# Low parts of the recurrent layer's weights made in the two feed-forward stages and kept in DRAM, that layer's elementwise products on VectorE alone

## The chip, the core and the metric

The kernel runs on one core of one Trainium2 chip. The metric is the device time of one execution in microseconds (us), the median of three runs. TensorE is called PE, VectorE DVE, ScalarE ACT, GpSimd POOL and SyncE SP in the profile's rows; PEld is PE's loading of weights.

## The reference

A chain of four layers on one sequence of 512 tokens with 1024 features, all in float32:

```
x = x + 0.5 * swiglu(rms_norm(x), gate, up, down)       # first feed-forward, 2816 wide
x = x + token_mixer(rms_norm(x))                        # short convolution beside a WKV-7 scan
x = x + 0.5 * swiglu(rms_norm(x), gate, up, down)       # second feed-forward
x = rms_norm(x)
x = x + fourier_attention(rms_norm(x)) @ w_out          # FFT mixing beside grouped attention
h = rms_norm(x)                                         # the recurrent layer (RG-LRU)
xr, gate = split(h @ w_in, 2)                           # 2048 each
xc = conv_b + sum_j shift(xr, j) * conv_w[j]            # 4 taps
for each direction:                                     # forward and reverse
    r = sigmoid(xc_block @ w_a + b_a);  i = sigmoid(xc_block @ w_x + b_x)    # 16 blocks of 128
    a = exp(-8 * r * softplus(-lam));   u = sqrt(1 - a*a) * i * xc
    hseq = scan(a, u)                                   # h[t] = a[t] * h[t-1] + u[t]
x = x + ((forward + reverse) * silu(gate)) @ w_out
y = rms_norm(x)
```

## The kernel before

Features lie on the 128 partitions, the 512 tokens along the free axis; a tile is 128x512 (256 KB). A weight group is 128x1024 (512 KB) and makes one 128x512 result out of eight tiles of input. Every product is made of three matmuls, to hold float32's precision on operands of a shorter type: `mm3` multiplies the high part of the weights with the high and the low part of the data, and the low part of the weights with the high part of the data. So `wload` does for each group: a DMA of the group into a tile `raw` (3 buffers), a cast into `wh` (4 buffers; on ACT or DVE, as the planner finds), and on DVE the difference `raw - wh` into `wl` (4 buffers). A group feeds 24 matmuls of 512 columns. `split` does the same to data (`h`, `l`).

The order of the instructions is made by a planner in the program (`Rec.schedule`): every operation is recorded with a cost, and a list scheduler plays the engines forward and takes, on each, the ready operation with the lowest priority number (its place in the program plus a bias). It holds back what lies more than 800 operations ahead of the oldest one not yet issued (`room`) and what finds no buffer free. An operation recorded by `nc.tt` may go to DVE or POOL, one by `nc.copy` to ACT or DVE, wherever it would end sooner by the planner's costs. To an operation of DVE or POOL that begins while the other is on SBUF, the planner adds 0.65 of the overlap. Each engine then runs its instructions strictly in that order, and all DMAs are issued by SP in one queue.

The four layers stand one after another in `Net.all`: `ffn`, `mixer`, `ffn`, `even` (Fourier and attention), `odd` (recurrent). In `ffn`, 22 pairs of groups (`_g`, `_u`) and 24 groups (`_d`) follow each other, in chunks of 8, 8 and 6 pairs with 8 groups behind each.

In `odd` a loop goes over eight blocks of 256 recurrent features. For a block, `conv` multiplies two groups of `o_in` and applies the taps (tiles `xc`), `gates` multiplies one group of `gw`, and makes, for two halves and two directions, the gates (Sigmoid, Tanh, Exp and Sqrt on ACT), products on the tiles `t` and the scan, and adds the directions; `silu` multiplies two more groups of `o_in` (tiles `z`), and `gated` multiplies and splits the result. `gates` of a block runs beside `conv` of the next. From the fifth block on, two groups of `o_out0` (`part`) stand in every turn; `out` uses the eight groups of `o_out1` at the end. That is 32 + 8 + 16 = 56 weight groups.

Of the kernel before, what the change touches and what calls it, by code (L numbers as in the profile page):

```python
# [8 lines left out]
F32 = mybir.dt.float32  # L9
F32R = mybir.dt.float32r  # L10
AF = mybir.ActivationFunctionType
ALU = mybir.AluOpType
# [221 lines left out]
class Rec:  # L234
# [22 lines left out]
    def add(self, eng, fn, args, kw, alts=()):  # L257
        o = Op()
# [35 lines left out]
        o.table = f if fn == "activation" and f in _FUNCS else None  # L294
        o.prio = o.seq + self.bias
        o.succ = []
        self.ops.append(o)
# [14 lines left out]
    def schedule(self, hold=2000.0):  # L312
# [30 lines left out]
        front = 0  # L343
# [18 lines left out]
        def room(o):  # L362
            if o.seq > front + self.ahead.get(o.fn, self.ahead[None]):
                return False
            for nm in o.touch:
                if nm in first and nm not in held:
                    t = self.tag[nm][0]
                    if free[t] <= 0:
                        return False
                    f = first[nm]  # L370
                    if f > front and use[t][front:f].max() >= self.size[t]:
                        return False
            return True
# [16 lines left out]
        while len(order) < n or ends:  # L390
# [14 lines left out]
            for e in engs:  # L405
# [85 lines left out]
                elif e in ports and o.port:  # L491
                    f = "gpsimd" if e == "vector" else "vector"
                    c += 0.65 * max(0.0, min(ports[f] - now, c))
                    ports[e] = now + c
# [146 lines left out]
class Net:  # L641
    def __init__(self, tc, a, ctx, wbufs=(3, 4, 4), slots=76):
# [10 lines left out]
        self.slots = slots  # L653
        self.late = 60
        nc = self.nc
        self.cst = self.cp.tile([128, _NC], F32, name="cst")
# [79 lines left out]
    def group(self, name, g):  # L736
        ap = self.a[name]
        return self.wload(ap[g], ap.shape[1:])

    def group_tm(self, g):  # L740
# [82 lines left out]
    def ffn(self, n):  # L823
# [3 lines left out]
        for ch, nk in enumerate((8, 8, 6)):  # L827
            hs = []
            for gi in range(g0, g0 + nk):
# [11 lines left out]
                nc.gpsimd.tensor_tensor(u, u, t, ALU.mult)  # L841
                hs.append(self.split(u))
            g0 += nk
            for m in range(8):
                wd = self.group(f"{n}_d{ch}", m)
                ps = self.P()
                self.gemm(ps, wd, hs)
                xm = self.x[m]
                nc.vector.scalar_tensor_tensor(xm, ps, 0.5, xm, op0=ALU.mult, op1=ALU.add)


# [683 lines left out]
    def odd(self):  # L1535
# [41 lines left out]
        def gates(g, xcs):  # L1577

            gw = self.wload(self.a["gw"][g], (128, 2, 4, 128))
            us = [(m, d, d * 16 + 2 * g + m) for m in range(2) for d in range(2)]  # L1580
# [13 lines left out]
            for (m, d, i), r, ig in zip(us, rs, igs):  # L1594
                th = self.T()
                A.activation(th, r, AF.Tanh, scale=c8[:, i:i + 1])
                nc.tt(ig, ig, xcs[m][0], ALU.mult)
                ths.append(th)
# [6 lines left out]
            for (m, d, i), r, ig, th in zip(us, rs, igs, ths):  # L1605
                A.activation(th, th, AF.Sqrt)
                nc.tt(ig, ig, th, ALU.mult)
                h = th
# [4 lines left out]
            for m in range(2):  # L1613
                nc.tt(ths[2 * m], ths[2 * m], ths[2 * m + 1], ALU.add)
            return ths[0], ths[2]

        def silu(b):
# [6 lines left out]
            A.activation(s, z, AF.Sigmoid)  # L1624
            nc.tt(s, s, z, ALU.mult)
            return s

        def gated(zs, hsum):
            out = []
            for s, h in zip(zs, hsum):  # L1630
                nc.tt(s, s, h, ALU.mult)
                out.append(self.split(s))
            return out
# [83 lines left out]

    def all(self):
        n = len(self.rec.ops)
        self.ffn("ffn1")  # L1720

        w = [o for o in self.rec.ops[n:] if o.fn == "dma_start"][:2]
        l = [o for o in self.rec.ops[:n] if o.fn == "dma_start"]
        for i, o in enumerate([l[0], w[0]] + l[1:3] + [w[1]] + l[3:]):
            o.prio = i - 100.0
        self.mixer()
        self.ffn("ffn2")
        self.even()
        self.odd()
# [21 lines left out]
```

## Time and profile before

| | before |
|---|---|
| median of three runs | 2006.84 us (2006.65 to 2007.8) |
| profiled execution | 2006.84 us |
| its span, first to last instruction | 2005.1 us |
| time outside the span | 1.74 us |
| mean granted TensorE clock | 0.979 of 2.4 GHz |
| PE busy in the span | 95% |
| first feed-forward, mixer, second feed-forward, Fourier and attention, recurrent layer | about 0 to 390, 390 to 830, 830 to 1195, 1195 to 1600, 1600 to 2005 us |

The profile shows one execution, instruction by instruction. An engine's row by stretch says how long it was busy, and how many instructions it began; a PE that is never idle at the full clock begins 443 matmuls of 512 columns in 100 us. All operations carry the line of one helper (L550, in the kernel after the change L551), so groups are told apart by the names of their tiles.

### The profile page before, as it was taken

To read this page: it belongs to the slowest core of one execution; us is meant where nothing else is said; L and a number is where in the kernel's file an instruction comes from. 1 tells how busy PE (TensorE), PEld (TensorE's weight loads), DVE (VectorE), ACT (ScalarE), POOL (GpSimd) and SP (SyncE) were. 2 spreads that over 40 slices of the span, in tenths; PEclk is the share of its full clock that TensorE was granted. 3 is DMA by queue.
4 is the path that set the end of the run, shared out by engine and by line. 5 is a ranking of instruction groups with operands and counts; after the bars stand their busy time and mean duration, and the time that the engine had idled before them with its cause. 6 is when DMAs were issued, how large, how long until landed. Compare 5 with 4: busy or idle time off the path is not lost.

```text
span 2005.1 us, 24763 instructions
## 1 busy us (share of the span) xinstructions
PE 1904.9 (95%) x9756; PEld 1559.7 (78%) x9756; DVE 1345.2 (67%) x2041; ACT 789.3 (39%) x1118; POOL 488.2 (24%) x307
## 2 busy tenths in 40 slices
PE   7999999999999998999999998999999999788997
PEld 6888888877777776788888886888998887577777
DVE  7434434779898964754344357754678868999995
ACT  5222222543442422432222234332465546865661
POOL 2201101231101301412011025100101026566563
PEclk9999999999999989999999999999999999898999
DMA  5332332432322311423223223222211131222221
GB/s 179 102 99 90 112 103 87 150 97 83 97 79 64 95 56 32 142 90 105 95 94 108 89 92 117 76 64 93 86 53 43 64 95 63 74 85 84 85 74 64
DMA packets 83013, 178.57 MB, mean 89 GB/s; under 512 B 27216, under 2 KB 39760, under 8 KB 82896
## 3 DMA queue, kind: packets, MB, share of 16 engines
q1 hardware_dynamic: 82896, 176.99, 27.9%
q8 instruction: 76, 1.25, 0.3%
q14 instruction: 41, 0.34, 0.1%
HBM read 169.10 MB, written 7.86 MB: 88 GB/s over the span
## 4 chain that ended last, share of the span: by engine, by line
PE 68%; DVE 23%; issue 4%; ACT 2%; POOL 1%; DMA 1%; POOLq 0%; SPq 0%; DVEq 0%; ACTq 0%
PE pm L550 65%; DVE t L550 5%; DVE wl L550 5%; PE pw L550 4%; DVE q L550 2%; DVE xc L550 2%; DVE l L550 2%; DVE u L550 1%; DVE wh L550 1%; DVE s L550 1%; ACT t L550 1%; DVE z L550 1%; POOL t L550 1%; ACT L550 0%; DVE x L550 0%
## 5 line engine op out<-in xcount | busy, mean ns | idle before, releaser
L550 PE MATMUL pm<-xh,wl 128*128 128x512 f32 x1488 | 556.7, 396 | 30.9 <-DVE wl L550 30.8
L550 ACT CAST wh<-raw 128x1024 fp32r<-128x1024 f32 (+1 forms) x255 | 264.6, 1039 | 816.5 <-PE pm L550 743.8
L550 PE MATMUL pm<-xh,wh 128*128 128x512 f32 x1488 | 557.3, 397 | 12.2 <-ACT xh L550 8.2
L550 PE MATMUL pm<-xl,wh 128*128 128x512 f32 x1488 | 555.8, 396 | 0.0
L550 POOL TENSOR_TENSOR t<-t,t 128x512 f32<-128x512 f32 x110 | 216.4, 1978 | 947.7 <-DVE t L550 772.7
L550 DVE TENSOR_TENSOR wl<-raw,wh 128x1024 fp32r<-128x1024 f32 (+1 forms) x303 | 400.1, 1323 | 22.8 <-ACT wh L550 18.5
L550 PEld LDWEIGHTS pm<-xh,wl 128*128 128x128 f32 x1488 | 282.1, 190 | 96.5 <-DVE wl L550 37.8
L550 PEld LDWEIGHTS pm<-xh,wh 128*128 128x128 f32 x1488 | 283.2, 191 | 75.3 <-ACT xh L550 8.2
L550 PEld LDWEIGHTS pm<-xl,wh 128*128 128x128 f32 x1488 | 282.8, 190 | 61.3 <-issue 1.1
L550 PE MATMUL pm<-h,wh 128*128 128x512 f32 (+2 forms) x844 | 311.2, 388 | 13.9 <-DVE t L550 8.0
L550 PE MATMUL pm<-h,wl 128*128 128x512 f32 (+2 forms) x844 | 310.8, 387 | 6.2 <-DVE wl L550 6.2
L550 PE MATMUL pm<-l,wh 128*128 128x512 f32 (+2 forms) x844 | 310.1, 386 | 2.1 <-DVE l L550 2.1
L550 DVE TENSOR_TENSOR t<-pm,rstd 128x512 f32<-128x512 f32 x146 | 99.5, 687 | 218.5 <-PE pm L550 216.3
L550 PEld LDWEIGHTS pm<-h,wh 128*128 128x128 f32 (+1 forms) x844 | 158.7, 190 | 48.7 <-DVE t L550 8.9
L550 PEld LDWEIGHTS pm<-h,wl 128*128 128x128 f32 (+1 forms) x844 | 159.3, 190 | 39.5 <-DVE wl L550 8.1
L550 PEld LDWEIGHTS pm<-l,wh 128*128 128x128 f32 (+1 forms) x844 | 158.7, 190 | 35.6 <-DVE l L550 5.1
L550 ACT ACT_TABLE_LOAD x82 | 105.2, 1283 | 19.1 <-DMA x<-xT 6.1
L550 DVE SCALAR_TENSOR_TENSOR x<-pm,x 128x512 f32<-128x512 f32 x48 | 33.1, 689 | 118.6 <-PE pm L550 118.4
L550 POOL TENSOR_TENSOR acc<-acc,sq 128x512 f32<-128x512 f32 x42 | 68.3, 1635 | 136.2 <-ACT sq L550 135.9
L550 DVE TENSOR_TENSOR x<-x,pm 128x512 f32<-128x512 f32 (+1 forms) x44 | 27.5, 635 | 63.9 <-PE pm L550 63.8
L550 DVE TENSOR_TENSOR_SCAN t<-t,t 128x512 f32<-128x512 f32 x32 | 66.6, 2130 | 2.4 <-POOL t L550 2.4
L550 ACT ACTIVATE t<-t 128x512 f32<-128x512 f32 x100 | 60.4, 629 | 14.5 <-DVE t L550 9.0
(246 smaller groups left out, 2246.4 us busy)
## 6 DMA issues: line engine op xcount, KB each, us to landing
raw<-ffn_g SPq DMA_DIRECT2D x44, 512.0 KB, 3.7
raw<-ffn_u SPq DMA_DIRECT2D x44, 512.0 KB, 3.5
raw<-w_in SPq DMA_DIRECT2D x42, 512.0 KB, 3.7
raw<-ffn_d SPq DMA_DIRECT2D x32, 512.0 KB, 3.6
raw<-o_in SPq DMA_DIRECT2D x32, 512.0 KB, 3.5
raw<-e_f SPq DMA_DIRECT2D x16, 512.0 KB, 3.6
raw<-e_out SPq DMA_DIRECT2D x16, 512.0 KB, 3.5
raw<-o_out SPq DMA_DIRECT2D x16, 512.0 KB, 3.5
```

The source lines that it names most:

```text
L550: o.ins = getattr(getattr(self.nc, o.eng), o.fn)(*o.args, **o.kw)
```

## The change

Fifty-six low parts are made ahead. `put_low` takes a group of the recurrent layer, does the whole of `wload` on it (in the buffers of the running stage, its priority put back by 40 places) and stores the tile `wl` in a DRAM tile `low`. In the first feed-forward stage 28 groups are treated so (4 of `o_in`, the 8 of `gw`, the 16 of `o_out`), in the second the other 28 of `o_in`: one behind each of the first 20 pairs, and one behind every second `_d` group of the first two chunks. In `odd`, `group` then finds the low part in `self.low` and calls `wload_low`: two DMAs (`raw`, and `wl` from DRAM, the second held to 200 operations ahead), the cast into `wh`, and no difference on DVE. The high part is still cast there.

All products of `odd` that `nc.tt` recorded are recorded on DVE alone. POOL keeps the additions of squares in the two norms. And the planner adds 0.95 instead of 0.65 of an overlap of DVE and POOL, in all layers.

```diff
-            if o.seq > front + self.ahead.get(o.fn, self.ahead[None]):
+            if o.seq > front + (o.far or self.ahead.get(o.fn, self.ahead[None])):
...
-                    c += 0.65 * max(0.0, min(ports[f] - now, c))
+                    c += 0.95 * max(0.0, min(ports[f] - now, c))
...
+        if (name, g) in self.low:
+            return self.wload_low(ap[g], self.low.pop((name, g)), ap.shape[1:])
         return self.wload(ap[g], ap.shape[1:])
+
+    def wload_low(self, ap, low, shape):
+        nc = self.nc
+        raw = self.wt(shape, F32, "raw")
+        nc.sync.dma_start(out=raw, in_=ap)
+        l = self.wt(shape, F32R, "wl")
+        nc.sync.dma_start(out=l.bitcast(F32), in_=low).far = 200
+        h = self.wt(shape, F32R, "wh")
+        nc.copy(h, raw)
+        return h, l
+
+    def put_low(self, n):
+        for name, g in self.later[:n]:
+            ap = self.a[name]
+            self.rec.bias = self.behind
+            _, l = self.wload(ap[g], ap.shape[1:])
+            t = self.dp.tile(list(ap.shape[1:]), F32, name=self.nm("low"))
+            self.nc.sync.dma_start(out=t, in_=l.bitcast(F32))
+            self.rec.bias = 0
+            self.low[name, g] = t
+        self.later = self.later[n:]
...
                 hs.append(self.split(u))
+                if gi < 20:
+                    self.put_low(1)
...
                 nc.vector.scalar_tensor_tensor(xm, ps, 0.5, xm, op0=ALU.mult, op1=ALU.add)
+                if ch < 2 and m % 2 == 1:
+                    self.put_low(1)
...
-            gw = self.wload(self.a["gw"][g], (128, 2, 4, 128))
+            gw = self.group("gw", g)
...
-                nc.tt(ig, ig, xcs[m][0], ALU.mult)
+                V.tensor_tensor(ig, ig, xcs[m][0], ALU.mult)
...
-                nc.tt(ig, ig, th, ALU.mult)
+                V.tensor_tensor(ig, ig, th, ALU.mult)
...
-                nc.tt(ths[2 * m], ths[2 * m], ths[2 * m + 1], ALU.add)
+                V.tensor_tensor(ths[2 * m], ths[2 * m], ths[2 * m + 1], ALU.add)
...
-            nc.tt(s, s, z, ALU.mult)
+            V.tensor_tensor(s, s, z, ALU.mult)
...
-                nc.tt(s, s, h, ALU.mult)
+                V.tensor_tensor(s, s, h, ALU.mult)
...
+        odd = [("o_in", g) for g in range(32)] + [("gw", g) for g in range(8)]
+        odd += [(f"o_out{h}", g) for h in range(2) for g in range(8)]
         n = len(self.rec.ops)
+        self.later = odd[28:]
         self.ffn("ffn1")
...
         self.mixer()
+        self.later = odd[:28]
         self.ffn("ffn2")
```

What this does to the order of the instructions is seen at three places; a name like `wl2701` is one buffer's use, the number behind `_` is the program's.

SP's queue in the first feed-forward stage, before: the loads of two groups for each pair, and nothing between them.

```order
L550 DMA raw90_165<-ffn1_u 128x1024
L550 DMA raw98_173<-ffn1_g 128x1024
L550 DMA raw102_177<-ffn1_u 128x1024
L550 DMA raw110_185<-ffn1_g 128x1024
L550 DMA raw114_189<-ffn1_u 128x1024
L550 DMA raw122_197<-ffn1_g 128x1024
```

The same place in the changed kernel:

```order
L551 DMA low101_176<-wl100_175 128x1024
L551 DMA raw114_189<-gw 128x1024
L551 DMA raw134_209<-ffn1_g 128x1024
L551 DMA raw138_213<-ffn1_u 128x1024
L551 DMA low117_192<-wl116_191 128x1024
L551 DMA raw130_205<-gw 128x1024
L551 DMA raw150_225<-ffn1_g 128x1024
L551 DMA raw154_229<-ffn1_u 128x1024
L551 DMA low133_208<-wl132_207 128x1024
```

Between two pairs stand the store of a low part and the load of the next group to be treated: four DMAs where there were two.

DVE in the third turn of the recurrent layer's loop, before, around the scans (printed here as SCALAR_TENSOR_TENSOR of two tiles t):

```order
L550 CAST wh2477_2565<-raw2476_2564 128x1024
L550 SCALAR_TENSOR_TENSOR t2409_2497<-t2394_2482,t2396_2484 128x512
L550 TENSOR_TENSOR t2427_2515<-pm2426_2514,rstd2285_2365 128x512
L550 TENSOR_TENSOR wl2478_2566<-raw2476_2564,wh2477_2565 128x1024
L550 SCALAR_TENSOR_TENSOR t2410_2498<-t2398_2486,t2400_2488 128x512
L550 SCALAR_TENSOR_TENSOR t2411_2499<-t2402_2490,t2404_2492 128x512
L550 SCALAR_TENSOR_TENSOR t2412_2500<-t2406_2494,t2408_2496 128x512
L550 TENSOR_TENSOR z2363_2451<-z2363_2451,t2409_2497 128x512
```

And in the changed kernel:

```order
L551 TENSOR_TENSOR t2620_2708<-t2620_2708,t2633_2721 128x512
L551 SCALAR_TENSOR_TENSOR t2633_2721<-t2618_2706,t2620_2708 128x512
L551 TENSOR_TENSOR t2624_2712<-t2624_2712,t2634_2722 128x512
L551 TENSOR_TENSOR t2628_2716<-t2628_2716,t2635_2723 128x512
L551 SCALAR_TENSOR_TENSOR t2634_2722<-t2622_2710,t2624_2712 128x512
L551 SCALAR_TENSOR_TENSOR t2635_2723<-t2626_2714,t2628_2716 128x512
L551 TENSOR_TENSOR t2632_2720<-t2632_2720,t2636_2724 128x512
L551 TENSOR_TENSOR t2633_2721<-t2633_2721,t2634_2722 128x512
L551 SCALAR_TENSOR_TENSOR t2636_2724<-t2630_2718,t2632_2720 128x512
L551 TENSOR_TENSOR z2646_2734<-z2646_2734,t2645_2733 128x512
L551 TENSOR_TENSOR t2635_2723<-t2635_2723,t2636_2724 128x512
L551 TENSOR_TENSOR z2652_2740<-z2652_2740,t2651_2739 128x512
```

The difference `wl` is gone from between the scans, and the products `t<-t,t` and `z<-z,t`, which stood on POOL, stand among them. In the whole program DVE's row of instructions has 104 products more, and POOL's 104 fewer.

SP's queue in the recurrent layer before, where a group of `gw` stands behind four of `o_in`:

```order
L550 DMA raw2449_2537<-gw 128x1024
L550 DMA raw2476_2564<-o_in 128x1024
L550 DMA raw2482_2570<-o_in 128x1024
L550 DMA raw2492_2580<-o_in 128x1024
L550 DMA raw2500_2588<-o_in 128x1024
L550 DMA raw2508_2596<-gw 128x1024
```

And at that place in the changed kernel:

```order
L551 DMA raw2716_2804<-o_in 128x1024
L551 DMA raw2724_2812<-o_in 128x1024
L551 DMA raw2732_2820<-gw 128x1024
L551 DMA raw2759_2847<-o_in 128x1024
L551 DMA wl2701_2789<-low1641_1718 128x1024
L551 DMA wl2707_2795<-low1653_1730 128x1024
L551 DMA wl2717_2805<-low1441_1518 128x1024
L551 DMA wl2725_2813<-low1453_1530 128x1024
L551 DMA wl2733_2821<-low165_240 128x1024
L551 DMA raw2765_2853<-o_in 128x1024
```

Four loads of `raw` stand ahead of five loads of `wl`; the first of these, `wl2701`, belongs to the group whose `raw2700` was loaded before all rows shown. Such runs stand at four places in the loop's first five turns; later the two kinds alternate.

## Rows read from the trace of the kernel before

**Rows 1.** The top of the page: busy time of each engine, its share of the span, instructions:

```profile
span 2005.1 us, 24763 instructions
...
PE 1904.9 (95%) x9756; PEld 1559.7 (78%) x9756; DVE 1345.2 (67%) x2041; ACT 789.3 (39%) x1118; POOL 488.2 (24%) x307
```

**Rows 2.** Busy time of each engine by stretch. Columns: the stretch in us from the span's start, its length, then for PE, PEld (weight loads), DVE, ACT and POOL the busy us and in brackets the instructions, then the granted TensorE clock (1.00 is 2.4 GHz), the busy share of the DMA engines and GB/s. The first stretch lies in the second feed-forward stage, the others in the recurrent layer:

```profile
900.00:1000.00 100.00, 100.00 (x443) 82.84 (x442) 40.69 (x47) 22.77 (x24) 11.09 (x5) 1.00 0.30 95
...
1657.00:1700.00 43.00, 40.94 (x173) 32.65 (x172) 40.21 (x35) 32.64 (x48) 27.65 (x16) 0.96 0.19 61
1700.00:1750.00 50.00, 34.15 (x138) 27.51 (x137) 48.00 (x48) 42.69 (x59) 27.71 (x15) 0.87 0.20 63
1750.00:1800.00 50.00, 46.81 (x203) 37.60 (x201) 49.13 (x42) 38.05 (x51) 32.32 (x17) 0.99 0.30 95
1800.00:1850.00 50.00, 40.89 (x154) 32.45 (x155) 46.86 (x41) 26.13 (x39) 32.62 (x18) 0.86 0.23 73
1850.00:1900.00 50.00, 45.31 (x193) 37.04 (x192) 45.42 (x44) 31.89 (x48) 26.20 (x15) 0.97 0.28 89
1900.00:1960.00 60.00, 53.25 (x223) 42.26 (x223) 58.20 (x46) 38.20 (x58) 44.69 (x24) 0.97 0.23 74
```

**Rows 3.** The same columns for the whole stretch in which the recurrent layer's loop runs:

```profile
1657.00:1960.00 303.00, 261.35 (x1077) 209.51 (x1076) 287.83 (x250) 209.60 (x298) 191.19 (x102) 0.94 0.24 76
```

**Rows 4.** Whom PE waited for in that stretch: waiting engine and tile, releaser, us in total, times, longest us:

```profile
PE pm L550 <- DVE wl L550: 28.9, 8, 11.4
PE pm L550 <- DVE t L550: 8.0, 2, 6.2
PE pm L550 <- ACT h L550: 2.4, 2, 1.5
```

**Rows 5.** DVE in the recurrent layer, 1630 to 1990 us, by form: out<-in, shapes, count, busy us, mean ns of one, idle time before them and its releaser:

```profile
L550 DVE TENSOR_TENSOR wl<-raw,wh 128x1024 fp32r<-128x1024 f32 x52 | 83.2, 1602 | 1.5 <-ACT wh L550 1.2
L550 DVE TENSOR_TENSOR_SCAN t<-t,t 128x512 f32<-128x512 f32 x32 | 66.6, 2130 | 2.4 <-POOL t L550 2.4
L550 DVE SCALAR_TENSOR_TENSOR xc<-t,vec,xc 128x511 f32<-128x511 f32 x32 | 35.4, 1115 | 0.2
L550 DVE CAST wh<-raw 128x1024 fp32r<-128x1024 f32 x27 | 24.4, 912 | 6.0 <-PE pm L550 6.0
L550 DVE TENSOR_TENSOR l<-z,h 128x512 fp32r<-128x512 f32 x16 | 22.7, 1423 | 0.0
L550 DVE TENSOR_TENSOR t<-pm,rstd 128x512 f32<-128x512 f32 x32 | 21.3, 679 | 8.6 <-PE pm L550 8.6
L550 DVE SCALAR_TENSOR_TENSOR t<-t,t 128x512 f32<-128x512 f32 x32 | 20.7, 682 | 2.9 <-ACT t L550 2.9
L550 DVE SCALAR_TENSOR_TENSOR xc<-t,vec,xc 128x510 f32<-128x510 f32 x16 | 17.0, 1064 | 0.3 <-ACT xc L550 0.3
L550 DVE TENSOR_TENSOR z<-z,t 128x512 f32<-128x512 f32 x7 | 12.0, 1718 | 0.0
L550 DVE TENSOR_TENSOR l<-xc,h 128x512 fp32r<-128x512 f32 x16 | 11.9, 750 | 0.1
L550 DVE TENSOR_TENSOR x<-x,pm 128x512 f32<-128x512 f32 x12 | 7.8, 675 | 0.0
```

**Rows 6.** POOL in the recurrent layer, 1600 to 2005 us, the same columns:

```profile
L550 POOL TENSOR_TENSOR t<-t,t 128x512 f32<-128x512 f32 x48 | 94.1, 1983 | 75.9 <-ACT t L550 74.7 <-DVE t L550 1.2
L550 POOL TENSOR_TENSOR t<-t,xc 128x512 f32<-128x512 f32 x31 | 53.5, 1749 | 38.2 <-ACT t L550 38.2
L550 POOL TENSOR_TENSOR z<-z,t 128x512 f32<-128x512 f32 x25 | 48.7, 1958 | 20.0 <-ACT z L550 19.9
```

**Rows 7.** DVE's instructions on the tiles t from 1600 us on: count, shortest, median and longest ns, first and last start:

```profile
L550 DVE SCALAR_TENSOR_TENSOR xc<-t,vec,xc x48: 735/743/1839, 1644.2 to 1905.7; 128x511 f32<-128x511 f32 x32, 128x510 f32<-128x510 f32 x16
...
L550 DVE TENSOR_TENSOR_SCAN t<-t,t x32: 1191/2245/2319, 1681.1 to 1953.5; 128x512 f32<-128x512 f32 x32
```

**Rows 8.** DVE in the second feed-forward stage, 900 to 1190 us, by form; POOL is mostly idle there:

```profile
L550 DVE TENSOR_TENSOR wl<-raw,wh 128x1024 fp32r<-128x1024 f32 x50 | 61.2, 1225 | 0.0
...
L550 DVE TENSOR_TENSOR l<-t,h 128x512 fp32r<-128x512 f32 x20 | 13.8, 692 | 0.7
```

**Rows 9.** ACT in the recurrent layer, 1630 to 1990 us, by form: the loads of function tables and the casts of weights:

```profile
L550 ACT ACT_TABLE_LOAD x33 | 42.3, 1283 | 0.5
...
L550 ACT CAST wh<-raw 128x1024 fp32r<-128x1024 f32 x25 | 25.9, 1048 | 38.5 <-PE pm L550 38.5
```

**Rows 10.** ACT's casts of weights in the second feed-forward stage, 900 to 1190 us:

```profile
L550 ACT CAST wh<-raw 128x1024 fp32r<-128x1024 f32 x49 | 51.6, 1054 | 200.5 <-PE pm L550 200.5
```

**Rows 11.** DMA issues of the whole run: out<-in, count, KB each, median us from issue to landing:

```profile
raw<-o_in SPq DMA_DIRECT2D x32, 512.0 KB, 3.5
...
xd<-x SPq DMA_DIRECT2D x8, 256.0 KB, 3.0
...
raw<-w_out_b SPq DMA_DIRECT2D x4, 512.0 KB, 7.4
```

**Rows 12.** The loads of the recurrent layer's first weights (o_in), us from issue to landing:

```profile
DMA to landing us min/median/max: 3.3/3.5/5.0
```

**Rows 13.** The stretch with the most DMA traffic, columns as in the second group:

```profile
10.00:20.00 10.00, 10.00 (x39) 7.52 (x38) 9.30 (x9) 8.62 (x14) 6.96 (x5) 1.00 0.78 309
```

More of the change, by code (lines that the diff above doesn't have):

```diff
@@ L295, in add @@
         o.prio = o.seq + self.bias
+        o.far = None
         o.succ = []
@@ L654, in __init__ @@
         self.late = 60
+        self.low, self.later, self.behind = {}, [], 40
         nc = self.nc
@@ L1725, in all @@
             o.prio = i - 100.0
+        assert not self.later
         self.mixer()
+        self.later = odd[:28]
         self.ffn("ffn2")
+        assert not self.later
         self.even()
```

## Prediction

> **What bounds the kernel now.** I read the top of the page first: PE is busy for 1904.9 of 2005.1 us [rows 1], so nearly all that can be won lies in the 100 us in which it is idle, and in stretches where its clock is below full. Then the busy time by stretch. In the second feed-forward stage PE is busy for all of 100 us and begins 443 matmuls, one in 0.2257 us, at the full clock, while DVE is busy for 40.69 us and ACT for 22.77 [rows 2]: PE alone bounds it. In the recurrent layer it is otherwise. From 1657 to 1960 us DVE is busy for 287.83 of 303 us, 95%, and PE begins 1077 matmuls [rows 3], which at 0.2257 us are 243.1 us of work. The shortfall of 59.9 us is idle time and a lower clock (0.86 and 0.87 of 2.4 GHz in the two stretches in which PE is idle most [rows 2]). The waits say the same: PE waits there mostly for DVE's `wl`, 28.9 us, with single waits of up to 11.4 us [rows 4]. DVE is late with everything, and `wl` is what PE notices.
>
> The forms tell why DVE is full. The 52 differences `wl` take 83.2 us, and nearly every DVE form with two operands in SBUF is long: a scan takes 2130 ns on average [rows 5] but 1191 ns at its shortest, the taps on `xc` 735 ns at the shortest and 1839 at the longest [rows 7]. Meanwhile POOL runs 104 products of 1.75 to 1.98 us [rows 6]. In the feed-forward stage, where POOL is little used, `wl` takes 1225 ns instead of 1602, and an `l` 692 ns [rows 5, 8], where `l<-z` in the recurrent layer takes 1423. So the two engines hinder each other, by about a microsecond for each meeting.
>
> **What is removed: DVE's load in the recurrent layer.** The forms shown sum to 323 us before [rows 5]. After: no `wl` (83.2 us gone); 32 scans at 1.19 (38.1 instead of 66.6) and 48 taps at 0.74 (35.5 instead of 52.4) [rows 7]; 16 `l<-z` at 0.69 (11.0 instead of 22.7) [rows 5, 8]; casts of weights, `t<-pm`, `t<-t,t`, `l<-xc` and `x` as before, 86.1 together [rows 5]. Added are the 104 products from POOL [rows 6], which join the few already on DVE to make 112; for one without POOL beside it I take the 0.692 us of an `l`, the same size and operands [rows 8]: 77.5 us instead of 12.0 and a little. Sum 248 us, so DVE's load falls to 248/323 of what it was: of the 287.83 us, 221 remain, 27.6 us for each of eight turns. The ends for a product are 0.68 us (the scalar form on two tiles `t` [rows 5]) and 1.72 (a product beside POOL [rows 5]); as POOL has nothing left there, the low end is near. At the high end the forms' sum would be 363 us, above the 323 of before, and nothing would be won.
>
> **What bounds the layer then.** Three engines have nearly the same load in a turn without `o_out`: DVE 27.6 us, ACT 209.6/8 = 26.2 us [rows 3], PE five groups of 24 matmuls, 27.1 us. ACT's load stays: its 33 table loads of 1283 ns and the casts of weights [rows 9] are still there (the order after has 32 of the casts on DVE instead of 31). Before, the fullest engine reached 95%; 27.6/0.95 is 29.1, and as now no engine has slack for the others' delays, I take 31 us for each of the first four turns. PE then falls short by 3.9 us in each, 15.6 together (ends: 0 where PE alone sets the turn, and 4 x 9 = 36 where a turn stays as long as a third cause makes it). In the last four turns two groups more make PE's load 37.9 us, and the others follow: the best stretch before held 203 matmuls, 45.8 us of work, in 50 us [rows 2], 3.2 us lost in 38 with DVE full; half of that, 1.6 us for each turn, 6.4 together.
>
> **The added wait for `wl` from DRAM.** Where DVE made the low part out of a tile that lay ready, SP now loads it: 3.5 us from issue to landing for 512 KB [rows 11], 3.3 to 5.0 in this layer [rows 12]. SP's order puts runs of `raw` loads ahead of runs of `wl` loads at four places, so the first `wl` of a run goes out once a buffer of `raw` is free, when PE has about one other group to do, 24 x 0.2257 = 5.4 us. Queued behind a waiting issue on SP are only more loads. At the busiest stretch the DMA engines moved 309 GB/s [rows 13], 1.7 us for 512 KB; behind one other load the `wl` lands after 3.5 + 1.7 = 5.2 us: just hidden. I take 0.5 us for each run, 2 us in all. The ends are 0 and, by the slowest load of this size in the trace, 7.4 us [rows 11], 2.0 us late for each run, 8 us.
>
> Here a rule of the Trainium skill speaks against the change: "HBM Reference", section Latency, gives an access 0.2 us on average and 2 us at high load. By it a load under traffic would land after some 3.5 + 1.8 + 1.7 = 7.0 us, an estimate from that page, 1.6 us late for each run, and the sum would be 4 us worse. The median of 3.5 us does not show it; the 7.4 us may.
>
> So the layer's shortfall of 59.9 us falls to 15.6 + 6.4 + 2 = 24: a gain of 36 us.
>
> **What is added to the feed-forward stages.** In each, 28 casts of 1.05 us [rows 10], 28 differences of 1.23 us [rows 8], 28 loads and 28 stores of 512 KB. Per 100 us, with 7.6 groups in some 370 us of stage, that is 8 us on ACT, 9.3 on DVE, and 7.9 MB more traffic: DVE would stand at 50, ACT at 31, the DMA engines at 0.30 x 174/95 = 0.55 [rows 2]. PE covers it. A store holds its buffer for some 3 us (the nearest row is `xd<-x`, half the size, 3.0 us [rows 11]). In SP's order a store waits for the difference just made, and behind it stand the next loads; those wait for buffers that the same difference frees, so the queue is not held up further. With a pair every 10.8 us, three buffers of `raw` and four of `wh` still bring a group to readiness some 9 us ahead of PE. Where the cover is thin, at the start and at the ends of six chunks, where PE waits for the last products, an extra cast or difference of 1.2 us can stand in the way: 0.5 us at each, 3 us in all. Ends: 0, and 1.2 us at each of the 56 places, 67 us, which would need the prefetch to be gone.
>
> **The 0.95.** It changes the planner's beliefs in every layer. Outside the recurrent layer POOL keeps its operations; a few stand elsewhere in its row. I take 0, with 5 us to either side: PE does fall short in the mixer too, and a new order may be better or worse.
>
> **Sum.** The profiled execution took 2006.84 us, 1.74 more than its span, and is the median itself. 2006.8 - 36 + 3 = 1974 us.
>
> **Rivals.**
> - *PE alone bounds the layer.* If the three engines interleave well, the first turns lose 2 us together instead of 15.6: 1960 us. For it: DVE's waits in this layer are short already [rows 5]. Against: three loads within 1.5 us of each other.
> - *ACT and the chain of a turn set its length.* Gates, tables, Exp, Sqrt, scan and split follow each other between ACT and DVE, and ACT reached 42.69 of 50 us in one stretch [rows 2]. Turns then stay at 36 us while no `o_out` is there: 4 x 8.9 = 36 us short instead of 15.6: 1994 us, and to 2000 if the later turns lose too.
> - *Nothing changes.* If DVE's long forms come from something other than POOL (the reads of loads, ACT's writes), the products cost 1.72 us each and take the place of `wl`: 2003 to 2011 us. Against it: 1225 against 1602 ns for one form in two stages.
> - *Slower: `wl` arrives late everywhere.* If loads with doubled traffic take the 7.4 us of the slowest row, each of the 45 groups in the loop is 2.0 us late at PE: 90 us, less the 2 counted: 2062 us. It decides from 36/45 = 0.8 us for each group. Against: four buffers, so a `wl` may be asked for three groups ahead.
>
> **How the numbers follow.** Chances: the forecast with its own range of 1963 to 1987, 0.54; PE alone (1950 to 1963), 0.12; the chain of a turn (1987 to 2002), 0.20; nothing (2003 to 2011), 0.07; late `wl`, 0.07. The likeliest gives 1974. A range from 1955 to 1999 leaves out part of the second, a little of the third and the last two: 2 in 10. About 0.2%, 4 us, is what a measurement of this kernel can tell from no change. Faster: 0.54 + 0.12 + 0.20 = 0.86; of the seven for nothing, six within 0.2% and one slower, with late `wl`: slower 0.08.
>
> **What would show it.** From the start of the loop to the last scan some 265 us instead of 303; DVE at 85% or less there; scans near 1.19, products near 0.69, no POOL but the norms; PE's clock above 0.95; no wait of PE for `wl` but short ones behind DMAs; the feed-forward stages at 443 matmuls in 100 us. A DVE still above 93%, PE waiting for `wl<-low`, scans above 1.5 us or PE idle in a feed-forward stage would make it wrong, each at the step named.

## The result, and the profile after

The changed kernel takes 1937.57 us (median of four, 1935.56 to 1939.01), the kernel before 2007.32 beside it on the same chip: a ratio of 0.9651 with a 95% interval of 0.9634 to 0.9667. The change wins 70 us. The prediction had the direction right, but the time lies 36 us below its 1974 and below the range, which began at 1955. The profiled execution's span went from 2005.1 to 1937.1 us.

The top of the page after the change (compare [rows 1]): busy time of each engine, share of the span, instructions.

```profile
span 1937.1 us, 25240 instructions
PE 1886.2 (97%) x9756; PEld 1552.9 (80%) x9756; DVE 1329.8 (69%) x2147; ACT 836.6 (43%) x1172; POOL 278.9 (14%) x203
```

Then busy time by stretch, in the columns of [rows 2]: first 100 us of the second feed-forward stage, in which low parts are made; then the recurrent layer's loop as a whole (it answers to [rows 3]); then its parts.

```profile
890.00:990.00 100.00, 100.00 (x443) 82.84 (x442) 50.69 (x57) 33.07 (x35) 10.60 (x5) 1.00 0.58 190
...
1643.00:1892.00 249.00, 244.64 (x1069) 201.04 (x1068) 207.70 (x307) 210.90 (x301) 0.00 (x0) 0.99 0.53 186
...
1664.00:1700.00 36.00, 35.17 (x156) 28.79 (x155) 31.79 (x46) 34.72 (x49) 0.00 (x0) 1.00 0.48 167
1700.00:1750.00 50.00, 48.08 (x204) 39.07 (x203) 45.62 (x70) 45.93 (x68) 0.00 (x0) 0.97 0.51 183
1750.00:1800.00 50.00, 48.40 (x213) 39.75 (x213) 43.05 (x63) 41.66 (x58) 0.00 (x0) 1.00 0.60 204
1800.00:1850.00 50.00, 50.00 (x222) 41.42 (x221) 35.82 (x55) 38.02 (x56) 0.00 (x0) 1.00 0.55 193
```

The loop took 303 us and takes 249. Its 1069 matmuls at 0.2257 us are 241.3 us of work, so 7.7 us are lost, where 59.9 were lost before and 24 were forecast. The feed-forward stage still begins 443 matmuls in 100 us. Of the 7.7 us lost, 5.9 lie between 1700 and 1800 us. PE is idle there for 3.5 us, in two waits for a load of a low part; the other 2.4 are matmuls that took longer than 0.2257 us, 2.0 of them in the stretch with a granted clock of 0.97. The first fence shows whom PE waited for in the loop (releaser, us in total, times, longest us), the second and third the chain that ended last, around the two waits (start us, us, what):

```profile
PE pm L551 <- DMA wl<-low: 3.5, 2, 1.9
PE pm L551 <- ACT t L551: 0.8, 1, 0.8
```

```profile
1689.95 12.03 PE pm L551 x53
...
1701.98 6.41 DMA wl<-low
```

```profile
1750.00 9.96 PE pm L551 x44
1759.96 6.78 DMA wl<-low
```

DVE's forms in the recurrent layer, 1615 to 1922 us, beside [rows 5]; scans and taps are nearly as short as their shortest was before [rows 7]:

```profile
L551 DVE TENSOR_TENSOR_SCAN t<-t,t 128x512 f32<-128x512 f32 x32 | 37.8, 1211 | 0.1
L551 DVE TENSOR_TENSOR t<-t,t 128x512 f32<-128x512 f32 x48 | 31.0, 682 | 6.7 <-ACT t L551 6.3
L551 DVE SCALAR_TENSOR_TENSOR xc<-t,vec,xc 128x511 f32<-128x511 f32 x32 | 23.2, 744 | 0.1
...
L551 DVE TENSOR_TENSOR t<-t,xc 128x512 f32<-128x512 f32 x32 | 21.5, 683 | 0.5 <-ACT t L551 0.4
...
L551 DVE SCALAR_TENSOR_TENSOR t<-t,t 128x512 f32<-128x512 f32 x32 | 21.2, 691 | 16.7 <-ACT t L551 16.6
...
L551 DVE CAST wh<-raw 128x1024 fp32r<-128x1024 f32 x29 | 20.0, 688 | 9.8 <-PE pm L551 9.6
```

### The profile page after: what moved, and what is told of

It is laid out like the page before. It is cut to its first block, busy times and chain, and to the rows that moved or that the text cites. A ratio compares the mean times of both kernels' runs of the same rounds, so it can differ in the third digit from the quotient of the medians.

```text
span 1937.1 us, 25240 instructions
## 1 busy us (share of the span) xinstructions
PE 1886.2 (97%) x9756; PEld 1552.9 (80%) x9756; DVE 1329.8 (69%) x2147; ACT 836.6 (43%) x1172; POOL 278.9 (14%) x203
## 4 chain that ended last, share of the span: by engine, by line
PE 81%; DVE 13%; ACT 2%; DMA 2%; issue 1%; SPq 1%; POOL 0%; POOLq 0%; DVEq 0%; ACTq 0%
PE pm L551 77%; PE pw L551 4%; DVE wl L551 2%; DVE q L551 2%; DVE t L551 2%; DVE u L551 1%; DVE l L551 1%; DVE s L551 1%; DMA wl<-low 1%; ACT t L551 1%; SPq L551 1%; DMA n<-dab 0%; DVE gt L551 0%; ACT L551 0%; DVE sh L551 0%
## 5 line engine op out<-in xcount | busy, mean ns | idle before, releaser
L551 PE MATMUL pm<-xh,wh 128*128 128x512 f32 x1488 | 500.2, 394 | 13.4 <-ACT xh L551 8.1
L551 PE MATMUL pm<-xh,wl 128*128 128x512 f32 x1488 | 500.5, 395 | 6.4 <-DMA wl<-low 3.5
L551 PE MATMUL pm<-xl,wh 128*128 128x512 f32 x1488 | 500.4, 395 | 0.0
L551 PE MATMUL pm<-h,wh 128*128 128x512 f32 (+1 forms) x844 | 282.9, 386 | 1.8 <-DVE yo L551 0.9
L551 PE MATMUL pm<-l,wh 128*128 128x512 f32 (+1 forms) x844 | 281.9, 385 | 2.1 <-DVE l L551 2.1
L551 PE MATMUL pm<-h,wl 128*128 128x512 f32 (+1 forms) x844 | 282.0, 385 | 1.3 <-DVE wl L551 1.3
L551 POOL TENSOR_TENSOR t<-t,t 128x512 f32<-128x512 f32 x62 | 116.9, 1886 | 880.4 <-DVE t L551 773.7
L551 PEld LDWEIGHTS pm<-h,wh 128*128 128x128 f32 x844 | 158.0, 189 | 35.0 <-DVE yo L551 1.3
L551 PEld LDWEIGHTS pm<-l,wh 128*128 128x128 f32 x844 | 158.0, 189 | 34.1 <-DVE l L551 4.0
L551 PEld LDWEIGHTS pm<-h,wl 128*128 128x128 f32 x844 | 158.5, 189 | 33.1 <-DVE wl L551 1.9
L551 ACT ACT_TABLE_LOAD x82 | 105.2, 1283 | 17.2 <-DVE s L551 8.2
L551 ACT ACTIVATE t<-t 128x512 f32<-128x512 f32 x100 | 60.6, 629 | 15.6 <-DVE t L551 9.9
```

Source lines behind the costliest of these rows:

```text
L551: o.ins = getattr(getattr(self.nc, o.eng), o.fn)(*o.args, **o.kw)
```

## The experiments

A table by stage tells where each kernel's time went. The borders are the first store of `xd`, the first load of x back from `xd`, the first `acc<-x` of the recurrent layer's first norm, and the last issue of `y`, all in the profiled execution (the 3 us behind the last issue are in no column); the last column is the median of the timed runs.

| kernel | ffn1 | mixer | ffn2 and even layer | recurrent layer | median |
|---|---|---|---|---|---|
| before | 349.2 | 468.9 | 780.3 | 403.8 | 2007.3 |
| after | 346.8 | 460.3 | 777.1 | 350.0 | 1937.6 |
| e1: after, 0.65 | 348.8 | 466.4 | 781.0 | 351.8 | 1952.8 |
| e2: before, 0.95 | 347.1 | 460.4 | 775.6 | 399.1 | 1986.9 |
| e3: products alone | 349.4 | 469.0 | 780.4 | 361.3 | 1963.6 |
| e4: low parts alone | 349.6 | 468.0 | 781.1 | 374.5 | 1976.6 |
| e5: far 800 | 347.0 | 459.6 | 773.7 | 366.7 | 1952.0 |
| e6: after, 0.80 | 348.5 | 477.7 | 780.9 | 348.3 | 1960.4 |
| e7: after, 1.10 | 347.0 | 473.0 | 771.6 | 347.6 | 1945.3 |
| e8: mixer's low parts | 347.1 | 522.7 | 774.3 | 352.5 | 2006.1 |
| e9: mixer's products | 346.8 | 461.9 | 778.2 | 349.1 | 1940.1 |
| e10: far 300 | 347.0 | 463.2 | 774.1 | 346.4 | 1935.8 |
| e11: far 120 | 347.2 | 464.2 | 777.0 | 367.6 | 1960.6 |
| e12: POOL beside | 346.7 | 460.9 | 775.5 | 365.2 | 1954.8 |

After, e5, e10, e11 and e12 differ in nothing before the end of the even layer; their mixers lie between 459.6 and 464.2, which is how far one execution's stage can be trusted.

### The three parts apart

**e1: the changed kernel with the planner's old number.**

```diff
-                    c += 0.95 * max(0.0, min(ports[f] - now, c))
+                    c += 0.65 * max(0.0, min(ports[f] - now, c))
```

> The changed kernel with the planner's 0.65 put back; low parts and products as changed. In the recurrent layer no product is left on POOL, so the planner's number should matter only in the other layers, where the changed kernel came out 14 us shorter than the kernel before. Theory A, the 0.95 gives those 14 us by a better order in the mixer and the attention: 1948 to 1952 us, with the recurrent layer as in the changed kernel. Theory B, they come from the low parts being made ahead and from where the stages begin: 1938 us, the same as the changed kernel.

1952.79 us, ratio 0.9727 (0.9712 to 0.9741): 15 us of the gain are the number's. The table shows where: not in the recurrent layer (351.8 against 350.0), but in the stages ahead of it, which have the same operations in both, in another order and with some casts on the other of ACT and DVE.

**e2: the kernel before with the new number alone**, the same line the other way.

> The kernel before with 0.95 in the planner and nothing else. Theory A: the mixer and the attention become 9 to 14 us shorter, 1993 to 1998 us. Theory B: 2007 us, within 3 us of the kernel before.

1986.90 us, ratio 0.9894 (0.988 to 0.9909): 15.3 us ahead of the recurrent layer (2.1 in ffn1, 8.5 in the mixer, 4.7 behind it) and 4.7 in it. The prediction's "0, with 5 us to either side" is wrong in a kernel where nothing but the planner's choices changed.

**e3: the kernel before with the recurrent layer's products on DVE**, low parts made on DVE as before.

```diff
-                nc.tt(ig, ig, xcs[m][0], ALU.mult)
+                V.tensor_tensor(ig, ig, xcs[m][0], ALU.mult)
...
-                nc.tt(ig, ig, th, ALU.mult)
+                V.tensor_tensor(ig, ig, th, ALU.mult)
...
```

> The kernel before with the recurrent layer's products on DVE alone; no low part is made ahead. Theory A, POOL's products lengthen DVE's operations about as much as they relieve it: the forms of DVE sum to 312 us instead of 323 (52 differences at 1.225 us more than the 248 worked out for the changed kernel), DVE stays full at 95%, the loop takes 292 us instead of 303: 1996 us. Rival, POOL relieves DVE and the long forms have another cause: 323 + 64 = 387 us of forms, a loop of 363 us, 2066 us.

1963.64 us, ratio 0.9778 (0.9763 to 0.9792), far below what I expected. The loop's row, whom PE waited for, and two forms of DVE (1630 to 1960 us):

```profile
1657.00:1919.00 262.00, 249.84 (x1080) 204.75 (x1080) 251.71 (x345) 204.69 (x299) 0.00 (x0) 0.97 0.27 87
```

```profile
PE pm L550 <- DVE wl L550: 12.2, 2, 6.5
```

```profile
L550 DVE TENSOR_TENSOR wl<-raw,wh 128x1024 fp32r<-128x1024 f32 x52 | 63.7, 1229 | 1.6 <-ACT wh L550 1.2
L550 DVE TENSOR_TENSOR_SCAN t<-t,t 128x512 f32<-128x512 f32 x32 | 37.3, 1209 | 0.0
```

DVE took over 104 products and stands at 251.7 of 262 us, 96%, as full as before. Yet PE loses 262 - 1080 x 0.2257 = 18.2 us instead of 59.9, and the recurrent layer is 42.5 us shorter. A DVE that is 95% busy was not in itself what PE paid for.

**e4: low parts alone**, with 0.65 and the products left to the planner: in the changed kernel, e1's edit, and e3's taken back.

> Low parts made ahead and loaded as in the changed kernel, the planner at 0.65, the recurrent layer's products left to the planner (most go to POOL). Theory A: 83 of 323 us of DVE's forms go, the meetings with POOL stay, DVE falls to 214 us of load and no longer fills the loop; the loop takes 255 to 262 us: 1955 to 1965 us. Rival, DVE and POOL take turns at SBUF so that POOL's products (191 us busy) and DVE's operations with two operands there hold the loop at 280 us or more: 1985 us. Scans stay near 2.1 us in both.

1976.59 us, ratio 0.9841 (0.9825 to 0.9858). The loop, whom PE waited for, and the scans:

```profile
1657.00:1929.00 272.00, 254.96 (x1073) 206.39 (x1072) 241.24 (x228) 199.60 (x288) 156.37 (x88) 0.96 0.49 170
```

```profile
PE pm L551 <- DVE t L551: 6.7, 2, 4.7
PE pm L551 <- ACT h L551: 4.5, 1, 4.5
PE pm L551 <- ACT t L551: 4.2, 3, 1.9
```

```profile
L551 DVE TENSOR_TENSOR_SCAN t<-t,t 128x512 f32<-128x512 f32 x32 | 69.0, 2211 | 2.3 <-POOL t L551 2.1
```

DVE has 83 us of differences less to make, is busy for 89%, and the loop loses 272 - 1073 x 0.2257 = 29.8 us, more than e3 with its 96%. PE no longer waits for `wl` but for the turn's own tiles, and the scans are at 2211 ns. Ahead of the recurrent layer the sum of the stages is 1598.7 us against 1598.4: making and storing 56 low parts cost nothing that shows.

In the recurrent layer the products alone give 42.5 us, the low parts alone 29.3, both with 0.65 (e1) 52.0 and not 71.8: each cures part of the same 59.9.

### What POOL does to DVE

**e12: products on POOL that nobody reads.** This asks whether POOL lengthened DVE's operations, or whether only the chain's own products on POOL were slow.

```diff
+        junk = self.cp.tile([128, 416], F32, name="junk")
...
                 xc[i] = [conv(2 * i), conv(2 * i + 1)]
+                for c in 6 * [xc[i][0][0], xc[i][1][0]]:
+                    G.tensor_tensor(junk, c[:, :416], c[:, :416], ALU.mult)
```

> The changed kernel, with 96 products added on POOL that nobody reads: in each of the eight turns of the recurrent layer twelve squares of the two xc tiles (128x416), into a tile of their own. DVE's own operations and the low parts stay as they are, so no operation of POOL stands in the chain of a turn. Before, 104 products of the chain ran there at 1.75 to 1.98 us. Theory H (an operation of POOL lengthens the operation of DVE beside it, and that is what cost the time before): scans go from 1211 ns to 1.6 to 2.2 us, products from 682 ns to over 0.9, the loop from 249 us to 265 to 290, total 1953 to 1978. Theory C (the time before went into the chain's own products on POOL, 1.75 us instead of 0.68, with the way from engine to engine; POOL beside DVE harms little): DVE's forms get longer, but the loop stays under 255 us and the total at 1936 to 1944. If POOL's products don't touch DVE's at all, scans stay at 1211 ns.

1954.80 us, ratio 0.9738 (0.9722 to 0.9754). The loop, and DVE's instructions on the tiles t (count, shortest, median and longest ns, first and last start):

```profile
1643.00:1906.00 263.00, 247.80 (x1065) 202.03 (x1064) 241.26 (x293) 215.86 (x307) 114.78 (x86) 0.98 0.52 177
```

```profile
L551 DVE TENSOR_TENSOR t<-t,t x48: 658/681/1365, 1661.5 to 1902.7; 128x512 f32<-128x512 f32 x48
L551 DVE TENSOR_TENSOR t<-pm,rstd x32: 672/678/692, 1626.4 to 1878.5; 128x512 f32<-128x512 f32 x32
...
L551 DVE SCALAR_TENSOR_TENSOR t<-t,t x32: 676/1361/1367, 1647.1 to 1892.1; 128x512 f32<-128x512 f32 x32
L551 DVE TENSOR_TENSOR_SCAN t<-t,t x32: 1192/1212/1897, 1663.4 to 1901.0; 128x512 f32<-128x512 f32 x32
```

Nobody reads what POOL makes, no engine waits for it in the loop, and still the recurrent layer is 15.2 us longer (365.2 against 350.0): the loop takes 263 us and loses 263 - 1065 x 0.2257 = 22.6 instead of 7.7. The total lies in theory H's range, at its cheap end, the loop just below H's 265 and well above C's 255. The scalar form on two tiles `t` takes 1361 ns in the median instead of 691; most scans stay short, as the squares wait only for `xc` and stand early in a turn. DVE's busy time in the loop rises from 207.7 to 241.3 us. PE's longest waits there are for ACT's `t` and `wh` (5.7 and 4.9 us) and not for DVE itself; and as the planner prices POOL's work too, part of the 15 us may be a new order. The run doesn't separate that.

What a meeting adds does not grow with the DVE form: here 0.67 us on a form of 0.69 us (691 to 1361 ns) and 0.7 us on a scan of 1.2 (1192 at its shortest, 1897 at its longest). In the kernel before, beside products of 512 columns, a scan went from 1191 ns at its shortest to 2245 in the median [rows 7], 1.05 us more, and a product took 1718 [rows 5], 1.04 us more than the 682 of after: the prediction's "about a microsecond for each meeting" was right there. So the price follows POOL's operation, which here has 416 columns and one tile as both operands; which of the two makes it cheaper is open.

The one form in the fence that reads PSUM, `t<-pm,rstd`, stays at 692 ns or below, where the product with both operands in SBUF takes up to 1365. The Trainium skill says this in "SBUF — State Buffer", section Who interferes with whom: a DVE instruction with two inputs in SBUF contends with a POOL instruction that reads SBUF, one with at most one such input, outside the two-port modes, does not. These rows agree.

This run has 114.8 us of POOL's work in the loop where the kernel before had 191.2 [rows 3]. Whether the rest of e3's 42.5 us is the same meeting or the chain's own products at 1.75 to 1.98 us instead of 0.68 [rows 6] was not separated.

### The planner's number

**e6 and e7: the changed kernel with 0.80 and 1.10** on the line of e1.

> The changed kernel with 0.80 in the planner. With 0.65 and 0.95 the stages ahead of the recurrent layer ended 13 us apart. Theory M, a higher price of an overlap is a better belief, so the gain grows with it: 1943 to 1948 us, between the two. Theory L, each number only makes another order, good or bad by chance: anywhere from 1930 to 1960 us, and not between the two if that falls so.

> The changed kernel with 1.10 in the planner. Theory M: as good as 0.95 or better, 1930 to 1939 us. Theory L: anywhere from 1930 to 1960 us.

1960.36 us (ratio 0.9772, 0.9747 to 0.9796) and 1945.32 (0.9687, 0.9673 to 0.9701). Over 0.65, 0.80, 0.95 and 1.10 the mixer lasts 466.4, 477.7, 460.3 and 473.0 us, up and down by more than its scatter, while the recurrent layer stays within 351.8 and 347.6. In ffn2 and the even layer the two larger numbers do better than the two smaller (777.1 and 771.6 against 781.0 and 780.9). So the 15 us are not a better belief paying more the nearer it comes to the truth: as far as four numbers can tell, the mixer's gain of 6 is an order that happened to be good. It is more than scatter all the same: the mixers of the four kernels with 0.65 last 466.4 to 469.0 us, of the six with 0.95 and the same operations 459.6 to 464.2. I found no one place for it: PE's waits in the mixer are spread over a dozen tiles, 28.0 us together before and 20.5 after, of which DVE's are 24.4 and 18.3.

### The loads of low parts

**e5, e10 and e11: the loads of low parts may run 800, 300 or 120 operations ahead** instead of 200.

```diff
-        nc.sync.dma_start(out=l.bitcast(F32), in_=low).far = 200
+        nc.sync.dma_start(out=l.bitcast(F32), in_=low).far = 800
```

> The changed kernel with the loads of low parts let out as far ahead as all others (800 operations instead of 200). In the changed kernel PE waits twice for such a load, 3.5 us in all, with a lower clock around it. Theory A, these waits come from the runs of loads in SP's queue, which 800 dissolves: both waits go, the loop falls from 249 to 243 to 246 us, 1931 to 1935 us in all. Rival, what PE loses there comes from the chain of a turn on ACT and DVE, and the load only lands last: within 2 us of the changed kernel.

1951.98 us, ratio 0.9721 (0.9707 to 0.9736); I expected neither. The chain at the border to the recurrent layer shows what went wrong:

```profile
1579.03 3.43 DMA raw<-e_out
1582.48 0.70 DVE wh L551
...
1588.08 5.79 PE pm L551 x24
1593.89 1.24 DVE wl L551
...
1595.17 5.96 PE pm L551 x24
1601.16 1.24 DVE wl L551
...
1602.44 5.78 PE pm L551 x24
1608.25 1.24 DVE wl L551
1609.50 3.55 DMA raw<-o_in
```

Three loads of low parts went out at 1538 to 1547 us, in the middle of the even layer's last groups, into three of the four `wl` buffers, which come free only when the recurrent layer has used them. With one buffer left, the even layer's groups went one by one: 24 matmuls, then a difference, then 24 matmuls.

> The changed kernel, with the loads of low parts allowed 300 operations ahead instead of 200. Nothing before the recurrent layer's first loads moves. In the changed kernel PE's sequencer waits twice for wl<-low, and the chain shows pieces of 6.4 and 6.8 us. If those two loads were late because they were asked for late, they come earlier: 1933 to 1937. If far 800 was slower because loads of low parts take the buffers of the stage before, 300 does some of that already: 1940 to 1948.

1935.80 us, ratio 0.964 (0.9625 to 0.9656), the best median of all, though its interval and that of the change overlap. The loop loses next to nothing, 246 - 1077 x 0.2257 = 2.9 us, and PE waits for no load there:

```profile
1643.00:1889.00 246.00, 245.03 (x1077) 201.55 (x1076) 210.30 (x315) 201.90 (x293) 0.00 (x0) 1.00 0.53 188
```

> The changed kernel, with the loads of low parts allowed 120 operations ahead instead of 200. The late-load theory (a wl<-low asked for late lands 3.5 to 5 us afterwards and PE waits the rest): PE waits for wl<-low in many groups, some 1 to 3 us in each of 45, 1960 to 2040. If buffers set the time of each load anyway, nothing moves: 1935 to 1940.

1960.64 us, ratio 0.977 (0.9754 to 0.9786): the recurrent layer is 17.6 us longer. Whom PE waited for there, and then whom SP's queue waited for:

```profile
PE pm L551 <- DMA wl<-low: 9.0, 6, 2.6
```

```profile
SPq L551 <- ACT wh L551: 111.5, 20, 11.5
SPq L551 <- DVE wh L551: 93.9, 20, 11.0
```

SP's queue no longer waits for PE to free buffers but for the casts. Six waits for loads, 9.0 us, are half of the 17.6; the rest was not taken apart. So the rival of the late `wl` exists, but much smaller than 90 us. In the recurrent layer of the profiled executions the window of 200 is 4 us short of the best (the medians don't tell 200 from 300), 120 costs 18, 800 costs 17 at the other end.

### Two attempts to go on

**e8: the mixer's weights too.** 28 of the mixer's groups get their low parts in ffn1, the recurrent layer keeps 36, made in ffn2.

```diff
-                if ch < 2 and m % 2 == 1:
+                if ch < 2 and (m % 2 == 1 or n == "ffn2"):
...
-        self.later = odd[28:]
+        self.later = [("w_in", t) for t in (4, 8, 0, 12, 16, 20, 5, 9, 1, 6, 10, 2, 7, 11, 3, 13, 17, 21, 26, 27, 34, 14, 18, 22, 28, 29, 30, 31)]
...
-        self.later = odd[:28]
+        self.later = odd[:36]
```

> The changed kernel with other low parts made ahead: in the first feed-forward stage 28 of the mixer's groups w_in, in the second 36 of the recurrent layer's (all of o_in and 4 of gw); the other 20 are made in that layer as before the change. If making them costs nothing in the feed-forward stages, the mixer, in which DVE is busy for 88 to 91 of 100 us, loses 34 us of DVE's work and gets 8 to 15 us shorter; the recurrent layer takes 25 us of differences back, and with DVE at 93% loses some 4 us: 1926 to 1934 us. Rival, the mixer is held by its chain of small steps and not by DVE's load: 1938 to 1945 us.

2006.12 us, ratio 0.9992 (0.9973 to 1.001): all of the gain is gone, 62 us in the mixer, and neither of my two ranges holds it. There PE waited, among others, for these (347 to 870 us), and the chain had these pieces:

```profile
PE pw L551 <- DVE yc L551: 14.7, 3, 9.1
PE pm L551 <- DMA wl<-low: 8.6, 2, 6.4
```

```profile
488.46 3.30 DMA dtt<-u
492.31 0.50 SPq L551
492.91 5.95 DMA wl<-low
...
593.69 1.74 DMA dtt<-u
596.05 0.45 SPq L551
596.54 6.53 DMA wl<-low
```

In the mixer SP's queue also carries stores that wait for DVE (`dtt<-u`), and a load of low parts behind one goes out when the store has gone, not when its buffer is free. The recurrent layer hardly misses the 20 low parts that it makes itself (352.5 us). The two waits for loads are only part of the 62 us. PE is idle in the mixer for 45 us instead of 21, and busy for 478 instead of 439 with as many matmuls (2776, 2772), at a granted clock of 0.93 instead of 0.97; what makes it wait was not taken apart further.

**e9: the mixer's products on DVE**, as in e3 but one stage earlier (`G.tensor_tensor` and `nc.tt` become `V.tensor_tensor`).

> The changed kernel, with the mixer's 66 or so products, sums and differences on POOL put on VectorE as well (the same step as in the recurrent layer, in another stage; nothing else is edited, so up to the mixer nothing can move). In the changed kernel the mixer lasts 460 us, DVE is busy for 371 of them and POOL for 92, and DVE's l<-gt,h takes 1131 ns beside POOL where l<-t,h takes 686. Theory P (operations of DVE beside POOL are what costs, a fuller DVE does not): the mixer shrinks by 6 to 20 us although DVE's busy share stays near 80 to 85%, total 1918 to 1932. Theory F (a DVE that is 90% busy in the mixer's middle is the bound, and more on it costs): 1940 to 1960. Theory L (the order that the planner happens on decides by up to 17 us either way): anything from 1920 to 1955, with the forms on DVE short all the same.

1940.12 us, ratio 0.9662 (0.9648 to 0.9677): no gain. `wl` fell from 1377 to 1217 ns in the mixer and POOL's busy time from 92 to 14 us, but the stage stayed at 461.9 us. Theory P (1918 to 1932) is out. PE's waits there add up to 23.9 us against 20.5 in the changed kernel; the two long ones are for a `wl` (7.9) and for `yc` (5.8), the others for small tiles, most of them DVE's. Why the shorter long operations bought nothing was not taken apart.

## Why the prediction was wrong

**What bounds the kernel, and where to look: right.** The largest gain, 53.8 of the span's 68 us, came from the recurrent layer, 52.2 of it from its loop's smaller loss. The reading that POOL and DVE hinder each other by about a microsecond for each meeting held too.

**DVE's load: nearly right.** Forecast 221 us, measured 207.7. The forms listed sum to 238 instead of 248: products 0.68 instead of 0.69, casts of weights 20.0 us instead of 24.4.

**"31 us for each of the first four turns": wrong, and the step that failed first.** It took 95% as a ceiling of the fullest engine and gave away 2 us more because three engines have like loads: 15.6 us, and 6.4 for the last four turns. Measured with no late load (e10) all eight turns lose 2.9 us. The rival "PE alone bounds the layer" was true of the loop, with a chance of 0.12; its 1960 us was too long as well, as it left the stages ahead as forecast. e3 shows why the rule was no good: with DVE at 96% PE lost a third of what it lost with DVE at 95% before. What went in e3 and stayed in e4 are the products on POOL with all that they lengthen (scans of 2.1 us, products of 1.7 to 2.0), and e12 says that lengthening DVE's operations alone costs some of it, as far as its new order does not. That a balanced set of short operations interleaves is my reading of these runs; no run shows it apart. In the prediction's own waits, DVE's `t` was already named with 6.2 us at once [rows 4], behind `wl`, and I read only the first row.

**"The 0.95: 0, with 5 us to either side": wrong by 15 us.** e1 and e2 agree. The number takes nothing from POOL outside the recurrent layer (203 instructions with either number in the changed kernel), but the order that it leads to is worth 6 to 8 us in the mixer, 2 in ffn1 and about 4 behind. With 0.80 (e6) the mixer is 11 us longer than with 0.65, so the sign was open too; a bound of 15 us to either side would have held.

**Feed-forward stages, +3 us: too dear.** Together with the mixer and the even layer, e4 adds 0.3 us to the kernel before. The store of a low part lands after 2.9 us in the median (forecast 3), PE stays at 443 matmuls in 100 us, DVE at 50.7 and ACT at 33.1 against the forecast 50 and 31.

**Late `wl`, 2 us: about half of what it was, within its ends of 0 and 8.** Two waits of PE, 3.5 us together, 4.8 us between e10's loss and this one's. The loads of low parts, 1600 to 1900 us (the row gives the issues, the last line their landings):

```profile
L551 SPq DMA_DIRECT2D wl<-low x53: 319/326/423, 1602.9 to 1894.8; - x53
...
DMA to landing us min/median/max: 3.1/4.1/8.4
```

The median is 4.1 us where 3.5 was taken; the two late ones took 6.4 and 6.8. Both were the first of a run of four issued within 4.1 us, right behind two loads of `raw`. This is the run at 1702:

```profile
L551 SPq DMA_DIRECT2D wl<-low x4: 319/382/423, 1702.0 to 1705.8; - x4
DMA to landing us min/median/max: 6.4/6.8/8.1
```

The two in the same 70 us that were issued alone, at 1719 and 1747, landed after 3.3 and 3.2 us. So the late loads are those in runs: the prediction put one other load ahead of the first `wl` of a run, 5.2 us and just hidden, where there were two, and three behind it. The estimate from the Trainium skill's "HBM Reference", section Latency, was 7.0 us and 4 us more in the sum: the two late loads stand near it, the median and the loads issued alone do not.

Summed against the forecast: 16.3 us from the turns and loads (a loss of 7.7 instead of 24), 17.2 from the stages ahead (14.2 gained instead of 3 lost), 1.6 from the ends of the recurrent layer: 35 us of the 36.

## What to carry to other kernels

An engine at 95% says that there is much to do on it, not what the engine that waits will lose: look at how long the single operations in the chain are, and whether a neighbour makes them long; moving work onto the full engine (e3) can win more than taking work from it (e4). When an edit changes what a planner believes, the order of every stage is drawn anew: give that term the spread of a few such orders, here 17 us in one stage, and not zero. A prefetch has a best distance: earlier takes buffers from the stage before, later shows its latency.

## What the runs showed that I had not expected

What a POOL product adds to the DVE operation beside it, where both of that operation's inputs lie in SBUF, is nearly the same for a short and a long form, and goes with the product: 0.67 and 0.7 us beside 416 columns of one tile squared (e12), 1.05 us on a scan and 1.04 on a product beside products of 512 columns [rows 5, 7]. With an operand in PSUM the form stays at 678 ns in the median, 692 at most. Loads of low parts (512 KB) land in the recurrent layer after 4.1 us in the median and 8.4 at the most, against 3.5 and 5.0 for its loads before [rows 12], at 186 instead of 76 GB/s in the loop [rows 3]; at the higher traffic a load issued alone still lands after 3.2 to 3.3 us, and the long ones stand in runs.
